# Token-major one-hots for the routing weights' scatter, with keys and weights stored four times each

## The chip, the cores and the metric

The kernel runs on one core of one Trainium2 chip. The metric is device time in microseconds of one execution, all inputs lying in HBM at its start. The engines are TensorE (PE, with its weight loads listed as PEld), VectorE (DVE), ScalarE (ACT), GpSimd (POOL) and SyncE (SP), which issues nearly all loads.

## What is computed

Two transformer blocks in float32 on 256 tokens of width 1024. The first has a pooling branch and a dilated attention; the second has two layers, a short convolution and a windowed attention, each followed by the same feed-forward part, a mixture of 16,384 tiny experts ("peer"). The change touches this part alone:

```python
def _peer(xn, w_q, subkeys, u_tab, v_tab):
    t = xn.reshape(-1, d)                                    # 256 tokens
    q = (t @ w_q).reshape(n_tok, 8, 2, 128)                  # 8 heads, 2 halves
    sc = jnp.einsum("thpd,hpnd->thpn", q, subkeys)
    sv, si = lax.top_k(sc, 16)                               # 16 best subkeys of each half
    cand = sv[:, :, 0, :, None] + sv[:, :, 1, None, :]       # 256 pairs of subkeys
    top_v, pos = lax.top_k(cand, 16)                         # 16 best pairs: 128 experts a token
    idx = ...                                                # key 0 * 128 + key 1 of each
    g = jax.nn.softmax(top_v, axis=-1)
    h = jnp.einsum("cd,ced->ce", xc, u_tab[idx])
    a = g * jax.nn.gelu(h)
    return jnp.einsum("ce,ced->cd", a, v_tab[idx])
```

## The kernel before

The kernel gathers no experts. In `peer` it multiplies all 256 tokens with all of `u_tab` (128 tiles of 128 experts), takes the gelu, multiplies by a dense matrix of routing weights that is zero outside a token's 128 chosen experts, and multiplies the result with all of `v_tab` (128 tiles again). Float32 precision comes from splitting each operand into two float32r parts, `hi` and `lo`: ScalarE casts a loaded weight tile to `hi` (line 121), VectorE or GpSimd subtracts to get `lo` (line 122), and TensorE makes three products for each pair (lines 132 to 134, or 1159 for `v_tab`). Instructions of an engine run in the order of its program; a priority offset puts the splits some steps ahead.

The large buffer X holds the activations of all experts, `[128 partitions, 128 tiles, 64 groups of four tokens, 4]`, float32, in two parts of 100 and 28 tiles (`xa`, `xb`). At the beginning of a layer the second part also holds the queries, in its tiles 0 to 15.

The loop over the 128 tiles of `u_tab` carries the routing beside it. During the first J1 = 40 steps its jobs run on VectorE: `lists` (the 16 best subkeys, values in `sv` and indices in `si`), `candidates`, `best`, `ranks`, `keys` (which looks subkeys up by a one-hot `e` of ranks), `weights`, and `turn`, once for each half of the tokens. In that part the `lo` subtractions go to GpSimd. `turn` transposes a half's keys and weights so that the 128 choices of a token lie along the partitions: `ij` holds key 0 and key 1 in float16, `gt[0]` and `gt[1]` the weight in two float16 parts.

From step 40 to step 124, 64 calls of `scatter` are spread over 84 steps, three or four steps with a call and then one without. A call does four tokens. VectorE compares an index ramp with the keys to get one-hots `o` of both keys (one instruction, line 1084) and multiplies the first key's by the weight's two parts (two instructions, line 1089). TensorE then forms, for each of the four tokens, the outer product over the 128 choices, `G[key 1, key 0]`, as two products of 128 columns (line 1094). VectorE multiplies finished tiles of X by G (line 1101), ScalarE copies G into those still to come (line 1104), which the later gelus are multiplied with (line 1135). The tiles `o` and `wi` have two buffers each, and G two PSUM banks.

In the kernel before, the token is the innermost index of `o` and `wi`, so the operands of a product step over four elements:

```python
                            PE.matmul(out=ps[:, t], lhsT=o[:, 1, :, t], rhs=wi[i][:, :, t],
                                      start=i == 0, stop=i == 1)
```

Of the kernel before, what the change touches and what calls it, by code (L numbers as in the profile page):

```python
# [10 lines left out]
F32 = mybir.dt.float32  # L11
F32R = mybir.dt.float32r
BF16 = mybir.dt.bfloat16
# [9 lines left out]
# The tokens stand in the order of (t % 4, t // 4 % 4, t // 16), in which a query's keys of the  # L23
# dilations 4 and 16 lie in its own half.
ORDER = np.arange(T).reshape(16, 4, 4).transpose(2, 1, 0).reshape(T)
# a head of two in a tile, its half of the partitions, and the other half
# [4 lines left out]
G_SCALE = 16384.0      # the routing weights' two float16 parts carry float32's significand  # L31
# how far ahead of their place in the program: splits of streamed weights, of kept ones, the norms
AHEAD, KEEP, CHAIN = 200, 100, 4000
HL = 3                 # streamed tiles in two parts at a time
WARM = 14              # products that start TensorE's clock while the first tokens load
RELIEF = 3             # splits behind a norm that leave VectorE to it
# peer: the tiles of U over which the routing ends and over which its weights are scattered, the
# tiles of V whose products for the second tokens come last, the tiles of X in its first part
# [12 lines left out]
def two_blocks(ctx: ExitStack, tc: tile.TileContext, io, out):  # L51
# [10 lines left out]
    def as_ordered(ap):  # L62
        """[128, T] in the sequence's order, read or written in ORDER's, and the other way round."""
        return ap.rearrange("p (c i j) -> p j i c", i=4, j=4)
# [21 lines left out]
    iota_4 = const.tile([P, P, 4], F16, name="iota_4")  # L86
    G.iota(iota_4, pattern=[[1, P], [0, 4]], base=0, channel_multiplier=0,
           allow_small_or_imprecise_dtypes=True)

# [5 lines left out]
    def fetch(src):  # L95
        """One tile on its way; where a phase has more room, every third in that."""
        fetched[0] += 1
        if more and fetched[0] % 3 == 1:
            raw = more[-1].tile([P, D], F32, tag="more", name="more")
        else:  # L100
            raw = stream.tile([P, D], F32, tag="raw", name="raw", bufs=4)
        SY.dma_start(out=raw, in_=src)
        return raw
# [21 lines left out]
    def in_order(dst, src):  # L125
        """A load behind the ones that stand before it: it may have to wait for its place."""
        tc.keep_in_program_order(SY.dma_start(out=dst, in_=src))
# [8 lines left out]
    def dense_t(src, acts, pool_share=0):  # L136
        """[128 columns of W, 256 tokens] of (tokens @ W), in PSUM; src: [128, 8, 128]."""
        ah, al = acts
        hi, lo = split(fetch(src), pool_share)
        ps = bank(p_mm, "mm")[:, :T]  # L140
        products(ps, [((hi[:, k * P:(k + 1) * P], lo[:, k * P:(k + 1) * P]), (ah[:, k], al[:, k]))
                      for k in range(8)], True, True)
        return ps

    def stacked(ps, dst):
        """Two heads' queries, over 8, in two parts: each head's first part in its half of the
        partitions, and its second in the other half."""
        for e, mine, _ in HALVES:
            S.activation(out=dst[mine, e], in_=ps[mine], func=AF.Copy, scale=0.125)
        for e, mine, other in HALVES:  # L150
            V.scalar_tensor_tensor(out=dst[other, e], in0=ps[mine], scalar=0.125,
                                   in1=dst[mine, e].bitcast(F32), op0=OP.mult, op1=OP.subtract)
# [4 lines left out]
    def keeper(pool, src):  # L157
        """keep(i): W's rows 128 i.. in their two parts, read once for both token tiles."""
# [11 lines left out]
    def rows_kept(act_of, keep, nxt):  # L170
        """x += the sum over 8 tiles of act[:, a]^T @ W's 128 rows: all of the first token tile, then
        all of the second beside the first one's next norm."""
# [19 lines left out]
    def last_rows(nxt, acc0, acc1, steps, scale=None):  # L192
        """The second token tile's last products, one half after the other, and around them the
        way from the first one's sums into the next layer."""
# [38 lines left out]
    def sum_squares(a, half, k=0, of=None):  # L233
        """64 * mean(x * x), one half of it."""
        of = of or x[:, a, half * 512:(half + 1) * 512]
        S.activation(out=squares, in_=of, func=AF.Square,  # L236
                     scale=0.25, accum_out=sums[a][:, k + half:k + half + 1])

    def mean_square(a):
        """64 * (mean(x * x) + eps)."""  # L240
# [5 lines left out]
    def inverse_root(a, m):  # L246
        """1 / sqrt(m / 64): Newton's steps r -> r * (3 - m * r * r) / 2, where each step's factor
        of 2 goes into the next step's m (64 * m, 16 * m, 4 * m)."""
# [14 lines left out]
    def spread(pool, src, tag="spread"):  # L263
        """A row of D parameters on all partitions."""
# [5 lines left out]
    class Enter:  # L270
        """The norm in front of a layer, and the products of the layer's first 512 columns, which run
        token tile by token tile: the first tile's while the second's sums are still open.
        take(a, sums [128 tokens, 512]); new(shape, type, name): a tile."""
# [32 lines left out]
        def both(self, a, r):  # L306
            """added and scaled in one."""
# [34 lines left out]
        def open(self):  # L342
            """Room for the products until the next layer has turned them."""
# [4 lines left out]
    class EnterConv(Enter):  # L348
        """Behind the first block: its closing norm and the convolution's, in one."""
# [18 lines left out]
        def inverse(self, a):  # L368
            """Of both norms: 1 / sqrt(mean(y * y) + eps * (mean(x * x) + eps)) with y = x * gain."""
# [13 lines left out]
    def turned(nat, n, which=p_tr):  # L383
        """n transposes of [128, 128], side by side in PSUM."""
# [8 lines left out]
    def split_act(pool, src, tag, bufs=1):  # L393
        """An SBUF tile [128, n] in two float32r parts."""
# [7 lines left out]
    def transpose_p(pool, pieces, name, bufs=None, which=p_acc):  # L402
        """Transposes of [128, 128] pieces, side by side."""
# [13 lines left out]
    # ------------------------------------------------------------------ first block  # L417
    def first_block(nxt):
        acts = xh, xl
        with ExitStack() as es:  # L420
# [66 lines left out]
            def window(g):  # L487
                """Windowed means minus the value."""
# [102 lines left out]
    def attention(acts, es1, at1, v_n, att, rest, loads):  # L591
        """Softmax over the keys of all three groups together."""
# [3 lines left out]
        # the first group's: per head a query's two parts, and over both the keys' first part  # L596
# [108 lines left out]
    # ------------------------------------------------------------------ second block  # L705
# [54 lines left out]
    def gqa_mixer(entered, nxt):  # L760
        acts, nat = (xh, xl), entered.nat
        with ExitStack() as es:
# [11 lines left out]
            def place_keys():  # L774
                """Each key head twice, over the queries' two parts."""
# [19 lines left out]
            def place(i):  # L795
                """Two heads of one key head: tile pair, partition half, tile, head."""
# [34 lines left out]
            def weighted(i, p_ts, pv):  # L831
                """Both key heads of a tile pair, each in its half of the partitions."""
# [91 lines left out]
    def peer(l, entered, nxt):  # L924
        acts, nat = (xh, xl), entered.nat
        with ExitStack() as es:
            with ExitStack() as es1:
# [10 lines left out]
                ij = kept.tile([P, 2, T], F16, name="ij")  # L938
                gt = [kept.tile([P, T], F16, name=f"gt{i}") for i in range(2)]
# [3 lines left out]
                # in the place of X's last parts  # L943
# [16 lines left out]
                def lists(n):  # L960
                    """The 16 best subkeys of one half of a head."""
# [22 lines left out]
                sv = [one.tile([P, 16, 16], F32, name=f"sv{a}") for a in range(2)]  # L984
                si = [one.tile([P, 16, 16], U32, name=f"si{a}") for a in range(2)]
# [55 lines left out]
                def keys(a, side, part):  # L1041
                    """The subkeys at these ranks, four heads at a time."""
                    hs = slice(part * 4, part * 4 + 4)
                    cs = slice(part * 64, part * 64 + 64)
                    e = one.tile([P, 64, 16], BF16, tag="e", name="e")
# [23 lines left out]
                def turn(a):  # L1069
# [5 lines left out]
                    S.copy(out=ij[:, :, s], in_=ps[:, 0:2 * P].rearrange("p (c t) -> p c t", c=2))  # L1075
                    g = ps[:, 2 * P:3 * P]
# [3 lines left out]
                def scatter(tg, done):  # L1080
                    """The weights of four tokens over all experts, [key 1, token, key 0]."""
                    s = slice(4 * tg, 4 * tg + 4)
                    o = two.tile([P, 2, P, 4], F16, tag="o", name="o")
                    V.tensor_tensor(out=o, in0=iota_4.unsqueeze(1).to_broadcast([P, 2, P, 4]),  # L1084
                                    in1=ij[:, :, s].unsqueeze(2).to_broadcast([P, 2, P, 4]),
                                    op=OP.is_equal)
                    wi = [two.tile([P, P, 4], F16, tag=f"wi{i}", name=f"wi{i}") for i in range(2)]
                    for i in range(2):
                        V.tensor_tensor(out=wi[i], in0=o[:, 0],
                                        in1=gt[i][:, s].unsqueeze(1).to_broadcast([P, P, 4]), op=OP.mult)  # L1090
                    ps = bank(p_tr, "G").rearrange("p (t i) -> p t i", t=4)
                    for t in range(4):
                        for i in range(2):
                            PE.matmul(out=ps[:, t], lhsT=o[:, 1, :, t], rhs=wi[i][:, :, t],  # L1094
# [86 lines left out]
    class Finish:  # L1181
        """The closing norm, from the last sums."""
# [48 lines left out]
def _bucket(rel, n_buckets, max_distance):  # L1231
    """T5 bucket of a relative position (a constant of the shapes)."""
# [11 lines left out]
def _layout(a):  # L1244
    f = np.float32

    def cols(w, n0, n1):
        """Tiles of 128 columns: [tile, 128 rows, row block, 128]."""
# [6 lines left out]
    def rows(w):  # L1255
        """Tiles of 512 columns: [tile, 4, 128 rows, row block, 512]."""
# [76 lines left out]
```

## Time and profile before

| | |
|---|---|
| time, median of 3 runs | 2212.88 us (2206.84 to 2214.99) |
| span of the profiled execution | 2210.8 us (no other time of that execution is given) |
| TensorE busy | 97% |
| VectorE busy | 71% |
| ScalarE busy | 49% |
| GpSimd busy | 16% |
| read from HBM | 370.44 MB, 168 GB/s over the span |

The profile is of one execution. Matmul records overlap, so the pace of TensorE is read from the distance of starts, and a record's own duration holds a fixed latency beside its columns. A group row reads: line, engine, operation, output from inputs, shapes and types, count, busy time and mean duration, then the engine's idle time before them and what ended it.

### The profile page before, as it was taken

The numbers are of one execution on the slowest core, as the hardware profiler recorded it, in microseconds if no ns is written. First come the engines' busy times: TensorE is split into PE (matmuls) and PEld (weight loads), VectorE is DVE, ScalarE is ACT, GpSimd is POOL, SyncE is SP. The second block draws the span as 40 slices with busy tenths as digits, with TensorE's granted clock in tenths as the row PEclk, the third lists the DMA queues.
The fourth block names the chain that finished last, engine by engine and source line by source line (L and its number), as shares of the span: only waits on it lengthen the run. The fifth ranks groups of instructions, "written<-read, shape, count | busy, mean of one in ns | idle before, by whom it ended". The sixth has DMA issues, their size and how long they took to land. (4 is left out here: it accounts for less than half of the span.)

```text
span 2210.8 us, 37689 instructions
## 1 busy us (share of the span) xinstructions
PE 2152.8 (97%) x14288; PEld 1961.3 (89%) x14288; DVE 1569.8 (71%) x3045; ACT 1074.3 (49%) x1975; POOL 353.3 (16%) x167
## 2 busy tenths in 40 slices
PE   8999999998999999999999999989999999999998
PEld 7999988998999999888888767989999999888887
DVE  4456777798577898555666686994788896565665
ACT  4556544344444444444455574444444444444454
POOL 3310101378300000000000232687000000000000
PEclk9999999999999999999999999999999999999999
DMA  6635746345544444665656652545444446556664
GB/s 245 209 124 175 236 130 195 115 153 159 166 144 152 144 145 153 190 192 191 192 194 201 214 180 71 159 144 180 144 145 151 144 144 190 191 191 191 192 193 139
DMA packets 104437, 373.94 MB, mean 169 GB/s; under 512 B 12096, under 2 KB 14144, under 8 KB 103744
## 3 DMA queue, kind: packets, MB, share of 16 engines
q1 hardware_dynamic: 103968, 371.01, 52.3%
q8 instruction: 112, 1.84, 0.3%
q14 instruction: 69, 0.57, 0.1%
q10 hardware_dynamic: 288, 0.52, 0.1%
HBM read 370.44 MB, written 1.05 MB: 168 GB/s over the span
## 5 line engine op out<-in xcount | busy, mean ns | idle before, releaser
L132 PE MATMUL mm<-xh,hi 128*128 128x256 f32 x2880 | 834.7, 290 | 21.8 <-ACT xa L1138 21.4
L133 PE MATMUL mm<-xl,hi 128*128 128x256 f32 x2880 | 817.7, 284 | 0.0
L134 PE MATMUL mm<-xh,lo 128*128 128x256 f32 x2880 | 817.1, 284 | 0.4 <-POOL lo L122 0.4
L121 ACT CAST hi<-raw 128x1024 fp32r<-128x1024 f32 x600 | 632.0, 1054 | 299.0 <-issue 138.8
L122 DVE TENSOR_TENSOR lo<-raw,hi 128x1024 fp32r<-128x1024 f32 x484 | 591.7, 1223 | 222.4 <-ACT hi L121 217.7
L132 PEld LDWEIGHTS mm<-xh,hi 128*128 128x128 f32 x2880 | 556.7, 193 | 24.7 <-ACT xa L1138 22.2
L133 PEld LDWEIGHTS mm<-xl,hi 128*128 128x128 f32 x2880 | 556.0, 193 | 0.3
L134 PEld LDWEIGHTS mm<-xh,lo 128*128 128x128 f32 x2880 | 554.6, 193 | 1.0 <-POOL lo L122 0.8
L1159 PE MATMUL acc<-hi,al 128*128 128x512 f32 x976 | 384.5, 394 | 0.0
L1159 PE MATMUL acc<-lo,ah 128*128 128x512 f32 x976 | 382.6, 392 | 0.0
L1159 PE MATMUL acc<-hi,ah 128*128 128x512 f32 x976 | 378.7, 388 | 0.0
L122 POOL TENSOR_TENSOR lo<-raw,hi 128x1024 fp32r<-128x1024 f32 x118 | 307.7, 2619 | 248.3 <-ACT hi L121 239.0
L1159 PEld LDWEIGHTS acc<-lo,ah 128*128 128x128 f32 x976 | 183.2, 188 | 42.8
L1159 PEld LDWEIGHTS acc<-hi,ah 128*128 128x128 f32 x976 | 183.2, 188 | 40.9
L1159 PEld LDWEIGHTS acc<-hi,al 128*128 128x128 f32 x976 | 183.5, 188 | 36.4
L1151 ACT CAST ah<-xa 128x256 fp32r<-128x256 f32 x200 | 81.3, 407 | 271.8 <-PE acc L1159 271.0
L1152 DVE TENSOR_TENSOR al<-xa,ah 128x256 fp32r<-128x256 f32 x200 | 84.9, 425 | 111.2 <-ACT ah L1151 111.2
L294 POOL TENSOR_TENSOR enl<-raw,enh 128x1024 fp32r<-128x1024 f32 x5 | 12.4, 2487 | 850.9 <-ACT enh L293 850.9
L1094 PE MATMUL G<-wi,o 128*128 128x128 f16 x1024 | 142.9, 296 | 0.0
L1084 DVE TENSOR_TENSOR o<-iota,ij 128x1024 f16<-128x1024 f16 x128 | 94.4, 739 | 58.7 <-PE G L1094 58.1
L1104 ACT COPY xa<-G 128x240 f32<-128x240 f32 (+22 forms) x92 | 35.4, 385 | 200.3 <-DVE xa L1101 153.5
L1101 DVE TENSOR_TENSOR xa<-G,xa 128x400 f32<-128x400 f32 (+31 forms) x128 | 111.8, 873 | 11.0 <-PE G L1094 11.0
(461 smaller groups left out, 2190.6 us busy)
## 6 DMA issues: line engine op xcount, KB each, us to landing
raw<-in_peer_u_dram SPq DMA_DIRECT2D x256, 512.0 KB, 3.5
raw<-in_peer_v_dram SPq DMA_DIRECT2D x256, 512.0 KB, 3.5
raw<-in_peer_w_q_dram SPq DMA_DIRECT2D x24, 512.0 KB, 3.7
raw<-in_conv_w_in_dram SPq DMA_DIRECT2D x20, 512.0 KB, 4.4
raw<-in_w_rest_dram SPq DMA_DIRECT2D x18, 512.0 KB, 3.6
raw<-in_w_qk_dram SPq DMA_DIRECT2D x16, 512.0 KB, 4.2
more<-in_w_rest_dram SPq DMA_DIRECT2D x10, 512.0 KB, 3.6
raw<-in_w_v_dram SPq DMA_DIRECT2D x8, 512.0 KB, 4.6
```

Of the source, the lines that this page charges most:

```text
L121: S.copy(out=hi, in_=raw)
L122: (G if on_pool else V).tensor_tensor(out=lo, in0=raw, in1=hi.bitcast(F32), op=OP.subtract)
L132: PE.matmul(out=ps, lhsT=ah, rhs=bh, start=first and i == 0, stop=False)
L133: PE.matmul(out=ps, lhsT=ah, rhs=bl, start=False, stop=False)
L134: PE.matmul(out=ps, lhsT=al, rhs=bh, start=False, stop=last and i == n - 1)
L1084: V.tensor_tensor(out=o, in0=iota_4.unsqueeze(1).to_broadcast([P, 2, P, 4]), in1=ij[:, :, s].unsqueeze(2).to_broadcast([P, 2, P, 4]), op=O ...
L1094: PE.matmul(out=ps[:, t], lhsT=o[:, 1, :, t], rhs=wi[i][:, :, t], start=i == 0, stop=i == 1)
L1101: V.tensor_tensor(out=dst[:, :, :old], in0=ps[:, :, i0:i0 + old], in1=dst[:, :, :old], op=OP.mult)
L1104: S.copy(out=dst[:, :, old:], in_=ps[:, :, i0 + old:i0 + n])
L1151: S.copy(out=act[0], in_=src)
L1152: V.tensor_tensor(out=act[1], in0=src, in1=act[0].bitcast(F32), op=OP.subtract)
L1159: PE.matmul(out=acc[a][half], lhsT=p[:, s], rhs=r[:, d], start=i == 0 and w == 0, stop=i == P - 1 and w == 2)
```

## The change

The tiles `o` and `wi` change their order from [expert, token] to [token, expert]. So that VectorE still finds runs of neighbouring elements in the broadcast operand, `turn` writes each key and each weight four times (`ij` and `gt` grow from 2 KB to 8 KB of each partition), and `scatter` reads the copies as the innermost four elements. The index ramp is stored once (`iota_k`) and not four times (`iota_4`). To make room, the lists `sv` and `si` and the one-hots `e` leave their own pool for tiles 16 to 21 of X's second part. `turn` issues two ScalarE copies where it issued one. The rest of the diff removes comments.

```diff
-    iota_4 = const.tile([P, P, 4], F16, name="iota_4")
-    G.iota(iota_4, pattern=[[1, P], [0, 4]], base=0, channel_multiplier=0,
+    iota_k = const.tile([P, P], F16, name="iota_k")
+    G.iota(iota_k, pattern=[[1, P]], base=0, channel_multiplier=0,
...
-                ij = kept.tile([P, 2, T], F16, name="ij")
-                gt = [kept.tile([P, T], F16, name=f"gt{i}") for i in range(2)]
+                ij = kept.tile([P, 64, 2, 4, 4], F16, name="ij")
+                gt = [kept.tile([P, T, 4], F16, name=f"gt{i}") for i in range(2)]
...
-                sv = [one.tile([P, 16, 16], F32, name=f"sv{a}") for a in range(2)]
-                si = [one.tile([P, 16, 16], U32, name=f"si{a}") for a in range(2)]
+                flat = X[1][:, 16:22].rearrange("p n g t -> p n (g t)")
+                sv = [flat[:, a].rearrange("p (n k) -> p n k", k=16) for a in range(2)]
+                si = [flat[:, 2 + a].bitcast(U32).rearrange("p (n k) -> p n k", k=16)
+                      for a in range(2)]
+                e = X[1][:, 20:22].rearrange("p n g t -> p (n g t)").bitcast(BF16).rearrange(
+                    "p (n k) -> p n k", k=16)
...
-                    e = one.tile([P, 64, 16], BF16, tag="e", name="e")
...
-                    S.copy(out=ij[:, :, s], in_=ps[:, 0:2 * P].rearrange("p (c t) -> p c t", c=2))
-                    g = ps[:, 2 * P:3 * P]
+                    for c in range(2):
+                        keys_c = ps[:, c * P:(c + 1) * P].rearrange("p (g t) -> p g t", t=4)
+                        S.copy(out=ij[:, 32 * a:32 * a + 32, c],
+                               in_=keys_c.unsqueeze(3).to_broadcast([P, 32, 4, 4]))
+                    g = ps[:, 2 * P:3 * P].unsqueeze(2).to_broadcast([P, P, 4])
                     V.tensor_copy(out=gt[0][:, s], in_=g)
                     V.tensor_tensor(out=gt[1][:, s], in0=g, in1=gt[0][:, s], op=OP.subtract)
...
-                    o = two.tile([P, 2, P, 4], F16, tag="o", name="o")
-                    V.tensor_tensor(out=o, in0=iota_4.unsqueeze(1).to_broadcast([P, 2, P, 4]),
-                                    in1=ij[:, :, s].unsqueeze(2).to_broadcast([P, 2, P, 4]),
-                                    op=OP.is_equal)
-                    wi = [two.tile([P, P, 4], F16, tag=f"wi{i}", name=f"wi{i}") for i in range(2)]
+                    fours = [P, 8, 32, 4]
+                    o = two.tile([P, 8, P], F16, tag="o", name="o")
+                    V.tensor_tensor(
+                        out=o.rearrange("p n (b c) -> p n b c", c=4),
+                        in0=iota_k.rearrange("p (b c) -> p b c", c=4).unsqueeze(1).to_broadcast(fours),
+                        in1=ij[:, tg].rearrange("p c t d -> p (c t) d").unsqueeze(2)
+                        .to_broadcast(fours), op=OP.is_equal)
+                    wi = [two.tile([P, 4, P], F16, tag=f"wi{i}", name=f"wi{i}") for i in range(2)]
                     for i in range(2):
-                        V.tensor_tensor(out=wi[i], in0=o[:, 0],
-                                        in1=gt[i][:, s].unsqueeze(1).to_broadcast([P, P, 4]), op=OP.mult)
+                        V.tensor_tensor(
+                            out=wi[i].rearrange("p n (b c) -> p n b c", c=4),
+                            in0=o[:, 0:4].rearrange("p n (b c) -> p n b c", c=4),
+                            in1=gt[i][:, s].unsqueeze(2).to_broadcast([P, 4, 32, 4]), op=OP.mult)
                     ps = bank(p_tr, "G").rearrange("p (t i) -> p t i", t=4)
                     for t in range(4):
                         for i in range(2):
-                            PE.matmul(out=ps[:, t], lhsT=o[:, 1, :, t], rhs=wi[i][:, :, t],
+                            PE.matmul(out=ps[:, t], lhsT=o[:, 4 + t], rhs=wi[i][:, t],
```

## Rows read from the trace of the kernel before

**Rows 1.** The page: span, busy time and share of each engine, and the busy tenths of two of them in 40 equal slices.

```profile
span 2210.8 us, 37689 instructions
PE 2152.8 (97%) x14288; PEld 1961.3 (89%) x14288; DVE 1569.8 (71%) x3045; ACT 1074.3 (49%) x1975; POOL 353.3 (16%) x167
PE   8999999998999999999999999989999999999998
DVE  4456777798577898555666686994788896565665
```

**Rows 2.** Busy time of each engine in stretches (us from the span's start): the two scatter stages. Each engine's busy us and instruction count, then the granted clock, DMA share and GB/s.

```profile
575.00:860.00 285.00, 285.00 (x2387) 281.63 (x2386) 238.24 (x411) 130.58 (x342) 1.72 (x1) 1.00 0.47 148
...
1560.00:1840.00 280.00, 280.00 (x2345) 276.79 (x2345) 235.97 (x406) 127.64 (x337) 0.00 (x0) 1.00 0.47 147
```

**Rows 3.** The timeline of TensorE's products around one scatter and at the next two: start, duration of the merged record, line, operation, operands, count.

```profile
701.81 0.28 PE L134 MATMUL mm<-xh,lo 128*128 128x256 f32 x1
701.94 1.12 PE L1094 MATMUL G<-wi,o 128*128 128x128 f16 x8
...
705.76 1.12 PE L1094 MATMUL G<-wi,o 128*128 128x128 f16 x8
...
712.46 1.12 PE L1094 MATMUL G<-wi,o 128*128 128x128 f16 x8
```

**Rows 4.** Single lines, products and weight loads: durations in ns (least/median/most), first and last start, shape.

```profile
L132 PEld LDWEIGHTS mm<-xh,hi x2880: 186/192/333, 30.8 to 1851.1; 128*128 128x128 f32 x192
L132 PE MATMUL mm<-xh,hi x2880: 276/283/583, 31.0 to 1851.2; 128*128 128x256 f32 x192
...
L1159 PE MATMUL acc<-hi,ah x976: 388/388/388, 889.4 to 2185.9; 128*128 128x512 f32 x196
...
L1094 PEld LDWEIGHTS <-o x1024: 115/116/133, 575.8 to 1834.0; 128*128 128x128 f16 x171
L1094 PE MATMUL G<-wi,o x1024: 288/297/299, 575.8 to 1834.1; 128*128 128x128 f16 x171
...
L1074 PEld LDWEIGHTS tr<-ident,key x8: 139/140/141, 512.2 to 1531.9; 128*128 128x128 f32 x8
```

**Rows 5.** The timeline of TensorE's products around the three transposes of the second turn of the first layer.

```profile
569.55 0.28 PE L134 MATMUL mm<-xh,lo 128*128 128x256 f32 x1
569.67 0.38 PE L1074 MATMUL tr<-ident,key 128*128 128x128 f32 x2
569.88 0.27 PE L1074 MATMUL tr<-ident,g 128*128 128x128 f32 x1
...
570.11 0.28 PE L133 MATMUL mm<-xl,hi 128*128 128x256 f32 x1
```

**Rows 6.** Groups of VectorE instructions between 580 and 870 us: busy us, mean ns of one, idle time before them and what ended it.

```profile
L122 DVE TENSOR_TENSOR lo<-raw,hi 128x1024 fp32r<-128x1024 f32 x81 | 98.7, 1219 | 12.9 <-ACT hi L121 12.9
L1089 DVE TENSOR_TENSOR wi<-o,gt 128x512 f16<-128x512 f16 x122 | 46.1, 421 | 0.5
L1084 DVE TENSOR_TENSOR o<-iota,ij 128x1024 f16<-128x1024 f16 x61 | 42.1, 689 | 29.2 <-PE G L1094 29.0
```

**Rows 7.** Groups of the whole span whose operands have 512 elements and come from PSUM.

```profile
L412 ACT COPY p_t<-tr 128x512 f32<-128x512 f32 x24 | 14.1, 588 | 13.8 <-PE tr L409 13.7
L325 DVE TENSOR_TENSOR xl<-tr,xh 128x512 fp32r<-128x512 f32 x20 | 13.3, 688 | 17.4 <-ACT xh L324 17.2
```

**Rows 8.** Busy time by stretch as in rows 2, from the start of every seventh scatter block of the first layer to the next (seven blocks and two steps without one; the stretches between are left out): the first, the last three, and the sum over all nine.

```profile
575.76:608.26 32.50, 32.50 (x275) 32.11 (x273) 24.90 (x46) 16.58 (x40) 0.96 (x1) 1.00 0.47 152
...
773.64:806.14 32.50, 32.50 (x275) 32.11 (x273) 28.59 (x48) 13.86 (x37) 0.00 (x0) 1.00 0.46 146
806.14:838.64 32.50, 32.50 (x275) 32.11 (x273) 30.23 (x54) 13.47 (x34) 0.00 (x0) 1.00 0.47 147
838.64:871.14 32.50, 32.50 (x275) 32.12 (x273) 30.71 (x53) 13.25 (x34) 0.00 (x0) 1.00 0.45 146
sum 295.38, PE 295.38 PEld 291.90 DVE 247.84 ACT 134.94 POOL 0.96; mean PE 32.82 PEld 32.43 DVE 27.54 ACT 14.99 POOL 0.11
```

**Rows 9.** The turn's copy on ScalarE (line 1075): durations in ns (least/median/most), first and last start, shape.

```profile
L1075 ACT CAST ij<-tr x4: 362/364/364, 513.6 to 1533.2; 128x256 f16<-128x256 f32 x4
```

**Rows 10.** The timeline around the second turn of the first layer, of VectorE and then of GpSimd.

```profile
571.42 0.29 DVE L1077 CAST gt<-tr 128x128 f16<-128x128 f32 x1 [28.33 <-ACT ij L1075]
571.62 1.97 DVE L1089 TENSOR_TENSOR wi<-o,gt 128x512 f16<-128x512 f16 x1
...
573.72 3.28 DVE L1089 TENSOR_TENSOR wi<-o,gt 128x512 f16<-128x512 f16 x3
...
570.92 2.40 POOL L122 TENSOR_TENSOR lo<-raw,hi 128x1024 fp32r<-128x1024 f32 x1 [0.49 <-ACT hi L121]
574.12 2.60 POOL L122 TENSOR_TENSOR lo<-raw,hi 128x1024 fp32r<-128x1024 f32 x1 [0.81 <-ACT hi L121]
```

**Rows 11.** The timeline of GpSimd at the beginning: the index ramp and the next work.

```profile
1.43 1.19 POOL L87 IOTA iota<- 128x512 f16 x1
11.46 1.28 POOL L299 TENSOR_TENSOR xn<-x,gain 128x512 f32<-128x512 f32 x1 [8.85 <-DMA x<-in_x_dram]
```

**Rows 12.** Groups of the whole span: an instruction of `lists`, and the copies of the queries into X.

```profile
L970 DVE FIND_INDEX8 si<-sv,sc 128x8 uint32<-128x128 f32 x64 | 18.5, 290 | 0.0
...
L952 ACT COPY xb<-mm 128x256 f32<-128x256 f32 x24 | 8.8, 367 | 0.0
```

## The prediction

> **What bounds the kernel now.** I read the page first: TensorE is busy for 97% of the span, VectorE for 71%, ScalarE for 49% [rows 1]. The row of 40 slices says more: TensorE is full nearly everywhere, and VectorE climbs from 7 to 9 tenths twice, in slices 12 to 15 and 29 to 33 [rows 1]. These are the stretches in which the routing weights are scattered, which is where the change works. The view of busy time by stretch confirms it: from 575 to 860 us and from 1560 to 1840 us TensorE is busy for every microsecond at a granted clock of 1.00, and VectorE for 84% of it, in either layer [rows 2]. So in the scatter stage the order of TensorE's products sets the time, and VectorE is the next engine in line.
>
> A busy TensorE is a modelled figure, so the pace has to be read from starts. In the timeline of one step the eight products of line 1094 start at 701.94, right behind the last dense product at 701.81, which is one normal step of 0.12; nothing is waited for [rows 3]. The next blocks start at 705.76 and 712.46 [rows 3]. The first distance, 3.82, is a step with a scatter; the second, 6.70, is a step with and a step without one, so a dense tile alone takes 2.88 (24 products of 0.12) and a block of eight scatter products costs 3.82 - 2.88 = 0.94, or 0.1175 each. There are 128 blocks: 120 us of the span, all of it on the path.
>
> **What a scatter product should cost.** The durations of single products separate a fixed latency from the streaming of columns. 256 clean columns take 283 ns, 512 take 388 [rows 4]: 105 ns for 256 columns, 0.41 ns for one, and a fixed 178. A scatter product takes 297 ns with only 128 columns [rows 4]: 119 ns of streaming where clean columns need 53. It reads both operands at a distance of four elements, since the tiles hold [expert, token] with the token innermost. Its weights are no slower for it: their load takes 116 ns against 192 for the float32 loads [rows 4]. So I put the excess on the strided moving operand.
>
> The Trainium skill speaks against this reading ("SBUF — State Buffer", section "Door 1: The DMA port swizzle"): a memory line is 16 bytes and two hits on it are enough for full rate; four 2-byte elements apart is exactly two hits, so the stride would be free and the products would stay at 0.94 a block. Row and page differ here: 119 ns against 53 is the measured side, though what the columns cost without the stride no run here shows. The Trainium skill ("TensorE: Matmul & The Clock Gate", section "Back-to-back issue gap") gives 81 ns for a sustained pair of weight load and 128 columns; by that an estimate of the saving would be 8 x 0.0365 x 128 = 37 us in place of the 51 below.
>
> **The change part by part.** (1) The products read contiguous columns and weights. A dense product's pace is 0.12 for 0.105 of columns, 0.015 over. With 0.053 of columns a scatter product comes to 0.068 and a block to 0.54: 0.40 less, 128 times: **51 us**. Bounds: the columns alone, 0.053, give a block of 0.42 and 67 us; the nearest contiguous products of 128 columns, the float32 transposes of line 1074, follow each other at 0.11 (three between 569.67 and the next dense product, which with its late follower makes 570.11 - 569.55 - 2 x 0.12 = 0.32) [rows 5], which gives a block of 0.86 and 10 us. I take 0.068, because the transposes' loads are float32 ones of 139 ns and more and the scatter's are of 116 [rows 4].
>
> (2) The three VectorE instructions stay three, of 1024, 512 and 512 float16 elements, with every operand's innermost run still contiguous (four copies in place of four tokens). They cost 689 and 421 ns today, 1024 elements in 689 where a float32 subtraction of 1024 takes 1219 [rows 6]. I take the same, nothing gained. The bound on the other side is float32's rate: 530 + 2 x 267 = 1.06 us more a scatter (512 elements at 688 [rows 7]); a rival below.
>
> (3) With TensorE faster, VectorE is the next limit. Between the starts of seven blocks and the next seven lie 32.50 us, and VectorE's busy time in them rises from 24.90 to 30.71 [rows 8]. After the change TensorE needs 32.50 - 7 x 0.40 = 29.7. The last two stretches hold 30.23 and 30.71 of VectorE's work, so there VectorE decides: 0.5 + 1.0 = 1.5 us lost if it is packed without gaps, 31.2 + 31.7 - 59.4 = 3.5 if it reaches 97%. The stretch before them (28.59) just fits. Today 29.0 us of VectorE's idle time in this stage stands in front of line 1084, until a scatter's products release its buffer [rows 6]; those come earlier, so this wait shrinks and can be used. I take 2.5 a layer, **5 us** back. The second layer has the same load [rows 2].
>
> (4) The turn in front of the scatters writes each value four times: two ScalarE copies of 512 elements (588 ns, line 412 [rows 7]) for one of 364 [rows 9], and on VectorE a cast and a subtraction of 512 from PSUM (688 for the one such row [rows 7], taken for both) for 128 at 290 each [rows 10]. Of the four turns the first of each layer lies far ahead. The second is close: VectorE idles 28.33 us for it, then casts at 571.42, and behind that cast wait the products with the weights, two of which the first scatter, 575.76 [rows 8], needs [rows 10]. The cast moves by 588 x 2 - 364 = 0.81 and takes 0.4 longer, the subtraction too. The first weighting then runs until GpSimd's split ends at 573.32, as it does now (571.62 to 573.59), and the second, at about 574.4 in place of 573.72, falls behind GpSimd's next split, 574.12 to 576.72; the three of 573.72 on, the last of them in its shadow, ended at 577.00 [rows 10]. It would end near 577.1, and TensorE would stand for up to 1.4. Behind the stalled weighting queue the next one-hots and the first subtraction of line 122; what waits for them is the next block, 3.4 later. Between 0 and 1.4 a layer: I take **2 us** for both.
>
> (5) Lists, indices and the one-hots `e` move into tiles 16 to 21 of X's second part. The same instructions run on other addresses; queries fill only tiles 0 to 15, and the scatters, the next to write there, come behind the turn anyway. Nothing, unless a wait appears (a rival). The index ramp is a quarter as long: GpSimd's 1.19 us shrink, but its next work, at 11.46, waits for a load [rows 11]. Nothing; without that cover it would be a gain of about 1.
>
> **The sum.** 51 - 5 - 2 = 44 us less. Against the profiled execution's span of 2210.8 [rows 1] that is 2167. The profile gives no other time for that execution; the median of the runs is 2212.9, 2.1 above the span, so I predict **2169 us**.
>
> **The rivals.** *Weight loads or another fixed pace hold the products at 0.11.* For it: every contiguous run of 128 columns in this trace goes at that pace [rows 5]. Against it: all of them load float32 weights. 10 - 2 = 8 less: 2205, no measurable change. *The stride costs nothing*: something else holds the products at 297 ns, the block stays, the turns cost 2: 2215. The 297 against a clean 231 speak against it. The Trainium skill's "SBUF — State Buffer", named above, would have it so. *The one-hots fall to one element per cycle.* Place: lines 1084 and 1089, 63 scatters in the 295.4 us of rows 8. VectorE's 247.8 us become 247.8 + 63 x 1.06 = 314.6, at 97% full 324, 29 more a layer, and TensorE waits for all of it: 2271, slower. It decides from 0.97 x 295.4 - 247.8 = 38.7 us, 0.6 a scatter. Against it stand the two-byte types and contiguous runs of four, which today run at 689 already. *The lists in X make the queries wait.* ScalarE's copies of the queries go to the same tile; if each waited for a list being written (ten VectorE instructions of about 0.29 [rows 12]), the 22 that have one before them could lose 22 x 2.9 = 64, less 44: 2233. It decides at 2 us a copy. Today's copies show no idle time before them [rows 12], and the regions are disjoint.
>
> **How the numbers follow.** Forecast 0.77, with its own range from 2153 (67 us less, 6 to 7 given back to VectorE, which then decides in the last three stretches too) to 2184 (a pace of 0.085: 33 less, 4 given back). A saving between that and the fixed pace, 2184 to 2201: 0.04. Fixed pace 0.08, free stride 0.03, one-hots slow 0.05, waits on the lists 0.03. The range, 2149 to 2197, holds the forecast and nearly all of the between. A measurement of this kernel tells about 0.5%, 11 us, from no change: faster 0.77 + 0.04 = 0.81, same 0.08 + 0.03 = 0.11, slower 0.05 + 0.03 = 0.08.
>
> **What would show it.** Right: products of line 1094 near 231 ns and 0.07 apart, blocks 3.42 and 6.30 apart, one-hots still near 690 and 420 ns, less idle time before line 1084, and in the last quarter of each scatter stage TensorE waiting on VectorE for a few us. The turn: ScalarE's two copies near 0.59, the first block of a layer up to 1.4 later behind its turn. Wrong: products still at 297 (the stride was not the cause), or at 231 and 0.11 apart (loads set the pace), one-hots near 1.2 us, or gaps before the query copies of line 952.

## The result

The changed kernel takes 2159.53 us (median; 2157.0 to 2162.85) against 2211.85 beside it: ratio 0.9758, 95% interval 0.9740 to 0.9776, so 52 us or 2.4% faster. Its profiled execution has a span of 2161.0, 49.8 less than [rows 1].

The page of the changed kernel, same parts as [rows 1]:

```profile
span 2161.0 us, 37694 instructions
PE 2100.8 (97%) x14288; PEld 1907.3 (88%) x14288; DVE 1573.3 (73%) x3045; ACT 1074.5 (50%) x1979; POOL 350.4 (16%) x167
...
DVE  4456778699488998665666685995889996566565
```

TensorE has lost 52 us of busy time, its weight loads 54, and nothing else has changed by more than 4. VectorE's work is the same to within 4 us and stands closer together in slices 12 to 16 and 29 to 33.

The timeline of TensorE around one scatter and at the next two, as in [rows 3]:

```profile
699.13 0.28 PE L134 MATMUL mm<-xh,lo 128*128 128x256 f32 x1
699.25 0.62 PE L1106 MATMUL G<-wi,o 128*128 128x128 f16 x8
699.68 0.36 PE L132 MATMUL mm<-xh,hi 128*128 128x256 f32 x1
...
702.63 0.62 PE L1106 MATMUL G<-wi,o 128*128 128x128 f16 x8
...
706.01 0.62 PE L1106 MATMUL G<-wi,o 128*128 128x128 f16 x8
```

Two blocks in neighbouring steps are 3.38 apart where they were 3.82, so a block costs 3.38 - 2.88 = 0.50, not 0.94. Its eight starts lie 56 ns apart in the median (118 before). From the first to the last of them pass 0.40 us, and 0.10 more until the dense products behind the block are back at their pace.

The products and their loads in the first layer alone: durations in ns (least/median/most), first and last start, to be read against [rows 4]:

```profile
L1106 PEld LDWEIGHTS <-o x512: 96/98/100, 575.3 to 845.8; 128*128 128x128 f16 x171
L1106 PE MATMUL G<-wi,o x512: 219/219/230, 575.3 to 845.8; 128*128 128x128 f16 x171
```

A product takes 219 ns in place of 297, a load 98 in place of 116. The stage from the first product to the last takes 270.5 us; before it took 296.2 (the starts of its first and last block lie 295.4 apart [rows 8]).

Where the 49.8 us came from: 128 blocks by 0.44 make 56.3; late blocks at the end of both scatter stages, below, take back 2.5 each, 4.9; that leaves 51.4. The other 1.6 lie outside the scatters, most of it (1.4) while the first layer's `v_tab` is multiplied, where the change has no instruction. This stretch takes 356.9 to 360.3 us in the traces of this case (365.5 in the run with the copies unused, below), so 1.4 is within its spread.

Busy time by stretch over seven blocks each, as in [rows 8] (the first, and the last three of the nine):

```profile
575.31:604.73 29.42, 29.42 (x274) 29.12 (x273) 24.30 (x45) 16.50 (x40) 1.02 (x1) 1.00 0.54 166
...
754.81:785.17 30.36, 29.94 (x275) 29.30 (x273) 28.67 (x46) 14.34 (x40) 0.00 (x0) 1.00 0.52 157
785.17:815.18 30.01, 29.85 (x275) 29.20 (x273) 29.77 (x54) 13.25 (x34) 0.00 (x0) 1.00 0.50 156
815.18:845.44 30.26, 29.86 (x275) 29.21 (x273) 30.02 (x54) 13.01 (x34) 0.00 (x0) 1.00 0.56 168
```

The first stretches take 29.42, 7 x 0.44 less than before. In the last three TensorE is no longer busy for all of the stretch, and VectorE is busy for 29.77 of 30.01 and 30.02 of 30.26.

One late block and what stood before it, TensorE first and then ScalarE:

```profile
838.06 0.28 PE L134 MATMUL mm<-xh,lo 128*128 128x256 f32 x1
838.19 0.62 PE L1106 MATMUL G<-wi,o 128*128 128x128 f16 x8
839.08 0.39 PE L132 MATMUL mm<-xh,hi 128*128 128x256 f32 x1 [0.27 <-ACT xb L1150]
...
837.54 0.23 ACT L1116 COPY xb<-G 128x40 f32<-128x40 f32 x1 [2.55 <-DVE xb L1113]
837.63 1.06 ACT L121 CAST hi<-raw 128x1024 fp32r<-128x1024 f32 x1
838.58 0.38 ACT L1146 ACTIVATE h<-mm 128x244 f32<-128x244 f32 x1
838.85 0.18 ACT L1150 ACTIVATE xb<-mm 128x12 f32<-128x12 f32 x1
```

The dense product at 839.08 starts 0.89 behind its block, where the one at 699.68 started 0.43 behind; it is 0.46 late, and the next block 0.49. It waits for a PSUM bank that ScalarE's gelu (line 1150) frees at 839.03; the gelu ran behind a cast, the cast behind a copy of G, and the copy had idled 2.55 us for VectorE's multiplication by the same block (line 1113). So the wait that ends last is ScalarE's, though VectorE looks full. Why the copy waits for the multiplication at all (both read the same block of G and write the same tile of X) no run here separates. Which of them makes the block late was the open question for the experiments.

### The profile page after: what moved, and what is told of

Read it like the earlier page. It is cut to its first block, busy times and chain, and to the rows that moved or that the text cites. A ratio compares the mean times of both kernels' runs of the same rounds, so it can differ in the third digit from the quotient of the medians.

```text
span 2161.0 us, 37694 instructions
## 1 busy us (share of the span) xinstructions
PE 2100.8 (97%) x14288; PEld 1907.3 (88%) x14288; DVE 1573.3 (73%) x3045; ACT 1074.5 (50%) x1979; POOL 350.4 (16%) x167
## 5 line engine op out<-in xcount | busy, mean ns | idle before, releaser
L1099 DVE TENSOR_TENSOR wi<-o,gt 128x512 f16<-128x512 f16 x256 | 106.4, 456 | 1.0
L1092 DVE TENSOR_TENSOR o<-iota_k,ij 128x1024 f16<-128x1024 f16 x128 | 94.6, 740 | 11.9 <-PE G L1106 10.7
```

The lines of the kernel that those rows point to most:

```text
L1092: V.tensor_tensor(out=o.rearrange("p n (b c) -> p n b c", c=4), in0=iota_k.rearrange("p (b c) -> p b c", c=4).unsqueeze(1).to_broadcast(fo ...
L1099: V.tensor_tensor(out=wi[i].rearrange("p n (b c) -> p n b c", c=4), in0=o[:, 0:4].rearrange("p n (b c) -> p n b c", c=4), in1=gt[i][:, s]. ...
```

## The experiments

**Which operand's distance cost what.** In three runs the scatter's products read the changed kernel's tiles four elements apart again, everything else as in the changed kernel; in a fourth the moving operand two apart.

```diff
+def apart(ap):                                  # four elements apart
+    return ap.rearrange("p t e -> p (t e)").rearrange("p (e t) -> p t e", t=4)
-  PE.matmul(out=ps[:, t], lhsT=o[:, 4 + t], rhs=wi[i][:, t],
+  PE.matmul(out=ps[:, t], lhsT=o[:, 4 + t], rhs=apart(wi[i])[:, t],             # e1
+  PE.matmul(out=ps[:, t], lhsT=apart(o[:, 4:8])[:, t], rhs=wi[i][:, t],         # e2
+  PE.matmul(out=ps[:, t], lhsT=apart(o[:, 4:8])[:, t], rhs=apart(wi[i])[:, t],  # e3
```

The moving operand alone:

> The changed kernel, but the scatter's products read their moving operand (wi) four elements apart again, the weights stay contiguous. Each product then takes other elements of the same tile, so G's entries stand in other places; shapes, counts and all other instructions stay. My theory, the moving operand's distance is the whole cost: products at 297 ns, blocks 0.94 us, the 52 us are gone, 2208 to 2214 us. The rival, the weights' distance: products stay at 219, blocks 0.50, 2156 to 2163. Both in part: in between, with a block between 0.50 and 0.94.

The weights alone:

> The changed kernel, but the weights (o's second key) are read four elements apart and the moving operand is contiguous (other elements of the same tile, as in the run with the moving operand apart). My theory: no change from the changed kernel, block 0.50, weight loads back at 116 ns in place of 98 or not, 2156 to 2163 us. The rival, the weights' distance set the pace: block 0.94, 2208 to 2214.

Both:

> The changed kernel with both operands four elements apart: all of the change but the contiguous reading (other elements of the same tile). If the products' reading is the whole gain, this is the kernel before: block 0.94, 2208 to 2216 us, and a difference from the kernel before prices the rest of the change (four copies, lists in the large buffer). If the one-hots' new order on VectorE or the lists bring part of it, it stays below 2205.

The moving operand two apart, within pairs of tokens:

> The changed kernel with the moving operand two elements apart, weights contiguous (other elements of the same tile). If a distance of four costs because only two of a line's elements are used, a distance of two uses four and should cost less or nothing: block 0.50 and 2156 to 2163 us. If any distance but one costs the same: block 0.94, 2208 to 2214. If the cost grows with the distance: block about 0.65 to 0.72, 2175 to 2190.

Loads and products of the first layer, in the order moving apart, weights apart, both apart, moving two apart:

```profile
L1106 PEld LDWEIGHTS <-o x512: 96/115/118, 573.8 to 868.2; 128*128 128x128 f16 x171
L1106 PE MATMUL G<-wi,o x512: 275/295/298, 573.8 to 868.3; 128*128 128x128 f16 x171
```
```profile
L1106 PEld LDWEIGHTS <-o x512: 112/113/136, 576.6 to 847.9; 128*128 128x128 f16 x171
L1106 PE MATMUL G<-wi,o x512: 219/219/249, 576.6 to 848.0; 128*128 128x128 f16 x171
```
```profile
L1106 PEld LDWEIGHTS <-o x512: 115/116/133, 576.9 to 873.0; 128*128 128x128 f16 x171
L1106 PE MATMUL G<-wi,o x512: 288/297/299, 576.9 to 873.1; 128*128 128x128 f16 x171
```
```profile
L1106 PEld LDWEIGHTS <-o x512: 95/96/100, 574.6 to 845.5; 128*128 128x128 f16 x171
L1106 PE MATMUL G<-wi,o x512: 217/219/231, 574.6 to 845.5; 128*128 128x128 f16 x171
```

| run | time (us) | ratio to the kernel before, 95% interval | stage, layer 1 |
|---|---|---|---|
| changed kernel | 2159.53 | 0.9758 (0.9740 to 0.9776) | 270.5 |
| moving four apart | 2206.76 | 0.9969 (0.9955 to 0.9984) | 294.5 |
| weights four apart | 2163.54 | 0.9771 (0.9748 to 0.9793) | 271.4 |
| both four apart | 2212.28 | 0.9991 (0.9981 to 1.0002) | 296.2 |
| moving two apart | 2163.25 | 0.9761 (0.9735 to 0.9787) | 270.9 |

The moving operand's distance is the cost: with it alone a product is back at 295 ns and a block at 0.91 (3.79 from block to block). The weights' distance makes the load 15 ns longer and a block 0.02 dearer (3.40). These 20 ns lie between the first product of a block and the second; the other six distances stay at 56 ns. With both, the stage is that of the kernel before to the tenth (296.2), the product that of [rows 4], and the whole kernel cannot be told from the kernel before: the four copies, the new place of the lists and VectorE's new order together are worth nothing by themselves, and the reading is the whole gain. Two elements apart costs next to nothing (blocks 3.39 apart, products 219 ns long and 58 from start to start); four apart doubles the distance of the starts, to 116. Of the three distances tried, one and two cost nearly the same and four does not, so the price is not one by the element. The time with the moving operand apart came out 1.2 us below its expected range, those with the weights apart and with two apart 0.5 and 0.3 above theirs, all less than the spread of the runs of one kernel.

**The one-hots without the four copies.** The changed kernel without the use of the four copies:

```diff
-  in1=ij[:, tg].rearrange("p c t d -> p (c t) d").unsqueeze(2).to_broadcast(fours)
+  in1=ij[:, tg].rearrange("p c t d -> p (c t) d")[:, :, 0:1].to_broadcast([P, 8, P])
-  in1=gt[i][:, s].unsqueeze(2).to_broadcast([P, 4, 32, 4])
+  in1=gt[i][:, s, 0:1].to_broadcast([P, 4, P])
```

> The changed kernel, but the one-hots and their weighting read one copy of each key and weight, the same element for all 128 places, and the ramp as one run; same results. The rival of the prediction in which VectorE falls to one element per cycle: one-hots 1.22 us for 0.69, weightings 0.69 for 0.42, 1.06 us a scatter or 67 a layer more on VectorE, which then sets the stage: 2260 to 2285 us. If a repeated single element keeps the rate: 2156 to 2163, and the fourfold storing is not needed.

Measured: 2238.69 us, ratio 1.0108 (1.0088 to 1.0129), 75 us over the changed kernel by the spans (2236.2). VectorE's groups between 580 and 870 us, as in [rows 6], and its busy time over most of the stage:

```profile
L1098 DVE TENSOR_TENSOR wi<-o,gt 128x512 f16<-128x512 f16 x115 | 74.5, 678 | 0.1
L1092 DVE TENSOR_TENSOR o<-iota_k,ij 128x1024 f16<-128x1024 f16 x58 | 69.8, 1211 | 0.0
```
```profile
577.13:875.00 297.87, 277.81 (x2422) 268.38 (x2421) 294.44 (x410) 135.46 (x345) 0.76 (x1) 0.98 0.47 144
```

This is the rival on the slower side, made real: 1211 ns for 689 and 678 for 421, as its price said, and VectorE busy for 294.4 of 297.9. So the copies are what the token-major layout needs: without them the change would have cost 24 us, 1.1%, clear of the runs' spread. The time is below the 2260 expected: the dense products of the last tiles run while the last blocks wait, so the 45.8 us by which the stage from first to last block is longer than the changed kernel's (316.3 and 270.5) are not all paid. Between the last block and the first product of `v_tab` only 3.6 us are left of the changed kernel's 17.5.

**The lists alone.** The kernel before with `sv`, `si` and `e` in the large buffer (the four lines of the diff that define them):

> The kernel before with only the lists, indices and one-hots of ranks moved into the large buffer. My step: nothing, within 3 us of the kernel before. The rival, that the query copies wait for the lists there: 10 to 60 us slower, gaps in front of the query copies on ScalarE.

Measured: 2214.72 us, ratio 1.0004 (0.9994 to 1.0015). The query copies as in [rows 12]:

```profile
L952 ACT COPY xb<-mm 128x256 f32<-128x256 f32 x24 | 8.8, 365 | 0.0
```

No idle time in front of them: the move costs nothing.

**What makes the late blocks late.** Four kernels. First, less work for VectorE:

```diff
-                    for i in range(2):
+                    for i in range(1):
                         V.tensor_tensor(out=wi[i]...
-                            PE.matmul(..., rhs=wi[i][:, t],
+                            PE.matmul(..., rhs=wi[0][:, t],
```

> The changed kernel without the second of the two VectorE multiplications of a scatter (both products read the first part, so the weights' second part is left out). It takes about 0.38 us a scatter from VectorE, 24 a layer, and nothing from TensorE. If VectorE decides the end of the scatter stage, the 2.5 us a layer that blocks come late there vanish: 3 to 6 us less than the changed kernel, 2153 to 2157. If something else makes them late (ScalarE, loads), nothing changes: 2158 to 2161.

Measured: 2156.87 us, ratio 0.9749 (0.9730 to 0.9768).

```profile
L1106 PE MATMUL G<-wi,o x512: 219/219/230, 575.0 to 844.1; 128*128 128x128 f16 x171
```

The stage is 269.0 us (from 575.04 to 844.08), so 1.5 of the 2.5 us are won, and 1.0 are still lost, although VectorE now has 24 us less to do. The changed kernel has seven late blocks in a layer. With less work the last four, those in the last two stretches, are late no more, and the three before them stay as they were (0.07, 0.39 and 0.46 for 0.10, 0.39 and 0.47). ScalarE's waits for VectorE at `xb` fall from 36.6 to 22.6 us and those at `xa` do not (74.7 for 71.9). Capacity alone does not explain the late blocks. Second, the same work with ScalarE's copies ahead:

```diff
+  if old < n:
+      S.copy(out=dst[:, :, old:], in_=ps[:, :, i0 + old:i0 + n])      # both parts of X first
   ...
   if old:
       V.tensor_tensor(out=dst[:, :, :old], in0=ps[:, :, i0:i0 + old], in1=dst[:, :, :old], op=OP.mult)
-  if old < n:
-      S.copy(out=dst[:, :, old:], in_=ps[:, :, i0 + old:i0 + n])
```

> The changed kernel with ScalarE's copies of a scatter's block issued ahead of VectorE's multiplications by it; same results. In the changed kernel ScalarE's copy waits up to 2.9 us for VectorE's reading of the same block, and the gelu and the next cast queue behind it. If that queue makes the blocks late: 2 to 5 us less than the changed kernel, 2154 to 2158. If VectorE's own work does, or the wait only changes sides: 2157 to 2164.

Measured: 2157.58 us, ratio 0.9741 (0.9725 to 0.9758), stage 268.1 us, every pair of blocks 3.38 or 6.26 apart. That interval overlaps the changed kernel's, so it ran again beside it, with two controls:

> The changed kernel itself, to stand on the same chip beside the next two. Ratio to the kernel before 0.974 to 0.978; scatter stage of 270.5 us a layer, 2.5 of them late blocks.

> The changed kernel with ScalarE's copies of a block issued ahead of VectorE's multiplications by it, once more beside the changed kernel. If ScalarE's queue made the blocks late: a stage of 268.1 us a layer again with no late block, 4 to 6 us less than the changed kernel beside it. If the first such run was luck: 0 to 2 us less.

> The changed kernel with the same 64 scatters spread unevenly over the same 84 steps: one in each step at first, about one in two at the end, so that VectorE's load is even; same results, the order of ScalarE's copies as in the changed kernel. If late blocks come from VectorE's load at the end of the stage: they vanish, 3 to 6 us less than the changed kernel. If they come from ScalarE's copies queueing behind VectorE wherever VectorE lags a little: blocks are late in other places, within 3 us of the changed kernel.

> The kernel before with the copies first. No block of it is late, so nothing can be won there: stage 296.2 us, within 3 us of the kernel before. A gain of 4 us or more would mean that the copies' place has a price besides the late blocks.

```diff
                 for tg in range(64):                              # e8 only
-                    at.setdefault(J1 + tg * (J2 - J1) // 64, []).append(tg)
+                    k = 0.238 / (J2 - J1)
+                    at.setdefault(J1 + int((1 - (1 - 4 * k * tg) ** 0.5) / (2 * k)), []).append(tg)
```

| run, all on one chip | time (us) | ratio to the kernel before, 95% interval | stage, layer 1 |
|---|---|---|---|
| changed kernel | 2161.3 | 0.9760 (0.9744 to 0.9777) | 270.5 |
| changed, copies first | 2158.2 | 0.9742 (0.9726 to 0.9758) | 268.1 |
| changed, earlier scatters | 2168.07 | 0.9794 (0.9780 to 0.9808) | 272.9 |
| before, copies first | 2212.69 | 0.9992 (0.9981 to 1.0004) | 296.2 |

The waits in the scatter stage of the changed kernel, of the one with the copies first and of the one with earlier scatters (us in total, times, longest us), each from one window that holds the stage:

```profile
ACT xa L1116 <- DVE xa L1113: 71.9, 36, 2.9
ACT xb L1116 <- DVE xb L1113: 36.6, 15, 2.8
```
```profile
ACT hi L121 <- PE mm L133: 125.1, 80, 1.9
DVE o L1092 <- PE G L1106: 18.9, 27, 1.9
```
```profile
ACT xa L1116 <- DVE xa L1113: 91.7, 46, 3.0
ACT xb L1116 <- DVE xb L1113: 18.9, 9, 2.5
```

With the copies first, ScalarE's 108 us of waiting for VectorE are gone; it now waits for dense products, and no product of TensorE waits for it. VectorE does the same work, and fits it. Its last two stretches there:

```profile
785.24:814.64 29.40, 29.40 (x275) 29.10 (x274) 29.40 (x54) 13.93 (x34) 0.00 (x0) 1.00 0.52 160
814.64:844.04 29.40, 29.40 (x275) 29.10 (x273) 29.40 (x53) 13.43 (x34) 0.00 (x0) 1.00 0.55 164
```

TensorE is busy throughout (29.40 of 29.40) beside a VectorE whose records leave no gap at all, and no block is late. So the late blocks came from ScalarE's queue behind VectorE, and VectorE's load bears on how long that queue is: less of it freed the last four blocks and not the three before. The even load of the earlier scatters moves the waits to `xa` and does not end them: 16 late blocks of the first layer sum to 4.8 us, the earliest in the sixteenth interval. The kernel before has no late block and gains nothing. Two traces show 2.4 us a layer for the copies' order, 4.9 in all; the medians lie 3.1 apart, less than the 4 to 6 expected, and the two intervals still overlap. So the traces show the copies' order as the cause of the late blocks; its gain in time is likely, but not shown. The kernel with the copies first has the lowest ratio of all kernels here, in both of its runs. Earlier scatters came out 6.8 us above the changed kernel beside it, outside both of its expected ranges: 2158.92 in its profiled execution and 2166 to 2171 in the others. That difference I cannot place, as only the quick one has a trace.

## Why the prediction was right, step by step

**The stride of the moving operand.** Right, by the two experiments with one operand each: 295 ns with the moving operand apart, 219 with the weights apart. The Trainium skill's rule ("SBUF — State Buffer", section "Door 1: The DMA port swizzle"), that two hits on a 16-byte line are enough, does not hold here: four 2-byte elements apart makes two hits and cost 76 ns in a product's record and 0.41 us in a block, two apart makes four hits and cost none and 0.01. The rival "the stride costs nothing" falls with it.

**The term of the sum that was mis-sized.** 51 us, measured 56. I had given a product the 15 ns by which a dense product exceeds its columns and put a block at 0.54; it costs 0.50, with 56 ns from start to start, 3 over the 53 of its columns. Dense products differ from these in type, columns and load (192 ns against 98), and which of the three makes their surplus no run here shows. The forecast also left out the 0.10 behind the last product, and the two errors nearly cancel: seven distances of 56 ns and 0.10 make 0.50, eight of 68 made 0.54. The rival "another fixed pace of 0.11" falls: the transposes' pace was theirs and not that of every 128 columns. Products at 231 were expected, 219 came: the fixed part of 178 ns, read from float32 products, does not carry over to these. So durations are a rough guide to the price: they fell by 78 ns, the starts moved together by 62.

**VectorE unchanged.** Right. Its groups between 580 and 840 us, as in [rows 6]:

```profile
L1099 DVE TENSOR_TENSOR wi<-o,gt 128x512 f16<-128x512 f16 x120 | 45.2, 418 | 0.5
L1092 DVE TENSOR_TENSOR o<-iota_k,ij 128x1024 f16<-128x1024 f16 x60 | 41.2, 687 | 4.1 <-PE G L1106 3.5
```

In the whole span the weightings take 106.4 us and the one-hots 94.6, against 104.2 and 94.4. The idle time before the one-hots shrank from 29.2 to 4.1 us, as forecast. Float32's rate was the right price for the layout without copies, as the run with the copies unused shows.

**The end of the stage.** The number was right, 5 us, and partly by luck. The forecast had the last two of nine stretches lose and the one before them just fit; that one loses most (30.36 - 29.42 = 0.94, the last two 0.59 and 0.84), with 28.67 us of VectorE's work in it. The mechanism was only half right. I let VectorE's busy time decide; what the late products waited for was ScalarE, in order behind a copy that waited for VectorE. VectorE's load does bear on the last two stretches, whose late blocks less work removed. But a sum of busy time would have said, wrongly, that only less work could help.

**The turn.** Wrong, 2 us, measured 0. VectorE and GpSimd around the second turn, to be read against [rows 10]:

```profile
542.33 5.17 DVE L1099 TENSOR_TENSOR wi<-o,gt 128x512 f16<-128x512 f16 x2
571.67 0.69 DVE L1084 CAST gt<-tr 128x512 f16<-128x512 f32 x1 [24.18 <-ACT ij L1081]
572.28 0.87 DVE L1099 TENSOR_TENSOR wi<-o,gt 128x512 f16<-128x512 f16 x1
573.08 0.68 DVE L1085 TENSOR_TENSOR gt<-tr,gt 128x512 f16<-128x512 f32 x1
573.68 0.41 DVE L1099 TENSOR_TENSOR wi<-o,gt 128x512 f16<-128x512 f16 x1
...
573.68 2.66 POOL L122 TENSOR_TENSOR lo<-raw,hi 128x1024 fp32r<-128x1024 f32 x1 [0.81 <-ACT hi L121]
```

The durations were as expected (0.69 and 0.68; the two ScalarE copies 588 each). The step that failed is what stands behind the turn. Each block has two weightings, in the blocks' order. In the kernel before all four of the first two blocks stood behind the turn's cast [rows 10], and I took that over. In the changed kernel VectorE's program has the first block's two ahead of it, at 542.33; those at 572.28 and 573.68 are the second block's, due at 578.69. So the first block waits for no part of the turn and stands where TensorE's order puts it, at 575.31, 6.09 us behind the first transpose, in both kernels. The weighting at 573.68 also escaped the collision: it starts in the same hundredth as GpSimd's split and takes 0.41. What moved the first pair ahead no run here shows.

Where the old order stays, the forecast holds. In the run with the copies unused the first block's weightings stand behind the cast again (VectorE, GpSimd, TensorE):

```profile
575.76 2.67 DVE L1098 TENSOR_TENSOR wi<-o,gt 128x512 f16<-128x512 f16 x1
575.50 2.39 POOL L122 TENSOR_TENSOR lo<-raw,hi 128x1024 fp32r<-128x1024 f32 x1 [0.81 <-ACT hi L121]
578.49 0.55 PE L1104 MATMUL G<-wi,o 128*128 128x128 f16 x7 [1.13 <-DVE wi L1098]
```

The second weighting takes 2.67 in place of 0.68 beside GpSimd's split, and the first block, begun at 577.13, goes on 1.3 us late; the forecast had 0 to 1.4.

**The lists.** Right, by the run with the lists alone.

The total of 44 less stands against 49.8 between the two profiled executions: 5 more from the blocks, 2 from the turn that cost nothing, less the 1.6 lost outside the scatters. The medians of the runs lie 52 apart; the 2.5 between these two measures lies within the spread of the runs.

## What to carry to other kernels

Separate a product's fixed time from its columns by two clean shapes of the same trace, and take the price itself from the starts. A product that streams more slowly than its columns may be reading its moving operand badly; here the layout of that operand was worth 0.41 us a block, that of the weights 0.02. When a vector engine has to write the better layout, keep the innermost run of every operand contiguous, by copies if need be: here the same layout without them was slower than doing nothing. Where two engines read one block, try issuing first for the engine that others queue behind. And a wait forecast from the order of the old trace holds only as long as the new program keeps that order.

## What the runs showed of the hardware that I had not expected

The moving operand's price is no price by the element: two 2-byte elements apart costs next to nothing (58 ns from start to start for 56), four apart doubles it (116). The weights four apart cost the load 15 ns and the stream 0.02 us a block. A float16 product of 128 contiguous columns with its own load starts every 56 ns within a block. The Trainium skill ("TensorE: Matmul & The Clock Gate", section "Back-to-back issue gap") has about 81 for such a pair in a sustained stream and about 56 for the isolated product; these streams of eight met the second figure. A VectorE multiplication of 512 float16 elements took 2.67 us in place of 0.68 when it started 0.26 behind a split on GpSimd, and 0.41, its usual time in the changed kernel, when it started with one. And VectorE's records can fill a stretch without a gap (29.40 of 29.40 us) while nothing waits for it.
